# Layer 0's sample values: four of eight samples moved from TensorE to VectorE

## The chip, the core and the metric

The kernel runs on one core of one Trainium2 chip. The time is device microseconds of that core, and the median of three runs is compared. A profile is one execution, taken by the hardware profiler, with every instruction's start and duration. Engines are named as in the profile: PE is TensorE (PEld its weight loads), DVE is VectorE, ACT is ScalarE, POOL is GpSimd, SP is SyncE, whose queue issues nearly all DMAs.

## The reference: what is computed

One inference step of a two-layer decoder. It runs on one prompt of 256 positions and on eight samples, each of one new position with 256 cached ones. Model width is 1024, feed-forward width 2816, and all is float32. Layer 0 mixes block-sparse attention (8 heads of 64) with a gated MLP over 128-position chunks. Layer 1 mixes stick-breaking attention with a causal pooling mixer. Each layer has an input projection, an output projection and a convolutional feed-forward, and every one of these runs for prompt and samples together.

The change touches the attention of the samples. With 256 cached positions, one past block of 256 is always kept, so layer 0's attention of a sample is a softmax over its 256 cached keys and its own key:

```python
past0 = gather_pages(cache_l0_kv, page_table)      # (8, 256, 2, 8, 64)
...
s = jnp.einsum('hqd,hqjsd->hqjs', qh, ks).astype(jnp.float32) * scale
s = jnp.where(mask, s, -jnp.inf)
p = jax.nn.softmax(s.reshape(H, qb, -1), axis=-1).reshape(s.shape)
return jnp.einsum('hqjs,hqjsd->qhd', p.astype(vs.dtype), vs)
```

The last line is the value product: for each sample and head, 256 weights times 256 cached rows of 64 values, plus the sample's own row.

## The kernel before

Tokens lie in columns and features on partitions: 264 columns, 256 of the prompt and 8 of the samples. Every float32 matrix is cut into a high part in TensorE's fast float32 format and the low rest. A product is three matmuls (high by high, high by low, low by high), and the three of one 128x128 weight block are a *block* below. Eight blocks are a *weight tile*. ScalarE makes its high half (`wh`, a copy) and VectorE its low half (`wl`, a subtraction), both in `split`, line 323. At a new tile, `split` traces tiles up to three ahead (`LOOK`), and each half has four buffers, so tile 24 needs the buffer of tile 20. Raw weights come by DMA in chunks of two tiles (`raw`), three chunks deep.

The phases follow each other on TensorE: `in0` (160 blocks, tiles 0 to 19), `out0` (64 blocks, tiles 20 to 27), `ff0`, `dn0`, then `in1`, `out1` (tiles 110 to 117), `ff1`, `dn1`. In an output projection, the first 16 blocks read catB (gated MLP or pooling) for four output tiles. From block 16 on catA (attention) is read, the sample columns included. The attention runs between the blocks: `blk(b, f)` calls `f` after block `b` of the phase. In `in0`, `out0`, `in1` and `out1` TensorE's instructions keep that order (`fixed`). On the other engines a planner orders the instructions before the run. Each engine takes the first in program order of those that the planner's own clock has ready, unless a dependency holds it: `keep_in_program_order` puts an instruction behind the one traced just before it on its engine, and `behind(i, j)` puts `i` behind `j`. `ahead[tt] = (a, b)` makes `split` put tile `tt`'s high half behind `a` and its low half behind `b`. SP's `late` DMAs keep program order.

For the samples, layer 0 does this. `sm_score` makes the scores of all eight, `sm_soft` the softmax (tile `psamp`, rows of heads and samples), `sm_tr` turns the weights and writes them into `PZ`. `sample_av` does the value product on TensorE with 32-column matmuls over two groups of four samples, and ScalarE copies the result into `msk`. In `out0`, `sm_out` turns that back (`po`), adds the own-key part `ob`, and cuts it into catA's sample columns. `v_turn` turns the prompt's values (`vtp`, copied to `vt` by ScalarE and VectorE, half each), `s_av` makes the prompt's attention (`pav`), and `halves` cuts it into catA.

Layer 1 already splits its samples. TensorE does 0 to 3 (`SPE` = 4). For samples 4 to 7, `zs_store` puts the weights into DRAM, `zs_spread` loads them back so that each of the 64 partitions of a head holds that head's 256 weights, and `zs_value` multiplies them with the cached values (laid out with positions along the row) and sums, 16 instructions on VectorE. Large tiles of all kinds share one pool of 24 slots (`up`).

Of the kernel before, what the change touches and what calls it, by code (L numbers as in the profile page):

```python
# [9 lines left out]
F32 = mybir.dt.float32  # L10
# [8 lines left out]
P = 128  # L19
# [144 lines left out]
def _consts():  # L164
# [38 lines left out]
    ("w", ((_NB - 16) * P * P,)), ("xw", (P * (KD + 16 * P + KD * T),)), ("x", (P, KD * T)), ("vec", (P, _NVEC)), ("cst", _CST_ARR.shape), ("rope", (P, 2 * T)), ("edge", (P, 384)),  # L203
    ("kt0", (NPHYS, P, 512)), ("vp0", (NPHYS, P, 512)), ("kt1", (NPHYS, P, 512)), ("vp1", (NPHYS, P, 512)), ("vt1", (NPHYS, P, 512)),
    ("cstate", (P, 2 * NF * 2 * NS)), ("pstate", (P, 4 * NS * 16)),
# [10 lines left out]
def tile_decoder_step(ctx: ExitStack, tc: tile.TileContext, a):  # L216
# [98 lines left out]
    def split(t):  # L315
        for tt in range(len(splits), min(t + (2 if t == 3 else LOOK), NT - 1) + 1):
            ci = chunk_of[tt]
            for c in range(ci, min(ci + 3, len(_CHUNKS))):
                raw(c)
            o = (tt * 8 - coff[ci]) * P  # L320
            src = raws[ci][:, o:o + 8 * P]
            h, l = splits[tt] = wtiles(tt)
            for i, j in zip((s.activation(h, src, AF.Copy), v.tensor_tensor(l, src, h.bitcast(F32), ALU.subtract)), ahead.pop(tt, ())):  # L323
                behind(i, j)
        return splits[t]
# [184 lines left out]

    last = [None]

    def halves(h, l, src, pin=False):
        i = s.activation(h, src, AF.Copy)
        if pin:
            tc.keep_in_program_order(i)
        v.tensor_tensor(l, src, h.bitcast(F32), ALU.subtract)

# [37 lines left out]

    def to_pz(src, fn, groups=2):

        for pg in range(NPG):
            x = src[:, pg * P:(pg + 1) * P].rearrange("p (t x) -> p t x", x=32)[:, :, :2 * NS].rearrange("p t (s c) -> p t s c", c=2)  # L560
            for gr in range(groups):
                s.activation(PZ[:, pg, 4 * gr:4 * gr + 4, NH * gr:NH * gr + NH].rearrange("p s (t c) -> p t s c", c=2), x[:, :, 4 * gr:4 * gr + 4], fn)

    def sample_av(st, pz, vtiles, name, groups=2):
        pv = at(f"pv_{name}")
        for gr in range(groups):
            for pg in range(NPG):
                for j in range(4):
                    sq = 4 * gr + j
                    pe.matmul(pv[32 * j:32 * j + 32, :], pz[:, pg, sq, :], vtiles[sq][:, pg, :],  # L570
                              start=gr + pg == 0, stop=gr + pg == groups + NPG - 2, skip_group_check=True)
        s.activation(st["msk"], pv, AF.Copy)
# [14 lines left out]
    def of_half(x, r):  # L587
        return x.rearrange("p t (g r s) -> p t r s g", g=2, r=2)[:, :, r]

    PZ = con.tile([P, NPG, NS, 32], F32, name="PZ")  # L590
    g.memset(PZ, 0.0)
# [13 lines left out]
    def v_turn(vt, src, ts, name, bank=None, e=None):  # L605
        n = len(ts)
        ps = turn([src[:, t, kb * P:(kb + 1) * P] for kb in range(2) for t in ts], f"vtp_{name}{ts[0]}", bank)
        for r, p in enumerate(ps):
            d, x = vt.rearrange("p b (t r d) -> p b t r d", r=2, d=HF)[:, :, ts[0]:ts[0] + n, r, :], p[:, :2 * n * HF].rearrange("p (b t d) -> p b t d", b=2, t=n)
            v.tensor_copy(d, x) if (e[r] if isinstance(e, tuple) else e) is v else s.activation(d, x, AF.Copy)  # L610

    def p_turn(dst, ws, name, pin=False, e=None, after=None, bank=None):
        ps = turn([w[:, i * P:(i + 1) * P] for w in ws for i in range(3)], name, bank)
        for r, p in enumerate(ps):
            d, x = dst.rearrange("p h (i r d) -> p (h i) r d", r=2, d=HF)[:, :, r, :], p[:, :6 * HF].rearrange("p (x d) -> p x d", d=HF)
            i = v.tensor_copy(d, x) if e is v else s.activation(d, x, AF.Copy)
            if pin:
                tc.keep_in_program_order(i)
            if after is not None:
                behind(i, after)  # L620
# [86 lines left out]
    def pick(xg):  # L707
        return lambda m, k: hl(xg, k)
# [120 lines left out]
    ktiles, kload = page_list(a["kt0"], "K0")  # L829
    vtiles, vload = page_list(a["vp0"], "V0")  # L830
    st0 = {}
# [80 lines left out]
    def sm_out():  # L912
        osam = sm.tile([P, 4, NS], F32, tag="osam", name="osam", bufs=1)
        v.tensor_tensor(osam, st0["ob"], v4[:, :, SEQ:T], ALU.mult)
        for b, r, po in sample_out(st0["msk"], "l0"):
            o = of_half(osam[b:b + 64], r)
            v.tensor_tensor(o, o, po, ALU.add)
        halves(catA[0][:, :, SEQ:T], catA[1][:, :, SEQ:T], osam)
# [45 lines left out]
    def gm_norm():  # L964
        Rb = rstd_of(st0["acc"], 1.0 / 512, "sgu", bank=mmb, w=onesr)
        for t in range(4):
            v.scalar_tensor_tensor(bv4[:, t, :], bv4[:, t, :], vec("sg")[:, t:t + 1], Rb, ALU.mult, ALU.mult)
        bvn = sm.tile([P, 4, NS], F32, tag="bvn", name="bvn", bufs=1)
        g.tensor_copy(bvn, bv4[:, :, SEQ:T])
        nc.sync.dma_start(a["bvn"], bvn)  # L970
        st0["vgt"] = f4("vgt", (P, 2, 512))
# [61 lines left out]
    blk(144, s_tr, 2)  # L1033
    blk(144, s_tr, 3)
    blk(152, gm_own)
    for t in range(4):
        blk(152, gm_gate, t)
    blk(159, lambda: sample_av(st0, PZ, vtiles, "l0"))
    run(orders["in0"], pick(xg), in0_evac, hk)
    nc.sync.dma_start(a["v0"], v4)  # L1040
    hk = Hooks()
    blk(4, sm_out)
    blk(4, lambda: v_turn(vt, v4, range(4), "v0", e=(s, v)))
    for t in range(4):
        blk(9, s_av, t)
# [116 lines left out]
    def zs_tr():  # L1162
        pP = mmb("pP1")
        for pg in range(NPG):
            pe.transpose(pP[:, pg * P:(pg + 1) * P], st1["zs"][:, pg * P:(pg + 1) * P], ident)
        to_pz(pP, AF.Copy, 1)
        st1["msk"] = f4("msk1", (P, 512))
# [6 lines left out]


    zsd = drp.tile([2 * (NS - SPE), 4, PAST], F32, name="zsd")
    spread = {}

    def zs_store():
        for t in range(4):  # L1180
            late(zsd[:, t], st1["zs"][32 * t + 2 * SPE:32 * t + 2 * NS, :])
        st1["osam"] = sm.tile([P, 4, NS], F32, tag="osam", name="osam1", bufs=1)

    def zs_spread(sq):
        pb = spread[sq] = f4(f"pb{sq}", (P, 4, PAST))
        for c in range(2):
            late(pb[64 * c:64 * c + 64], zsd[2 * (sq - SPE) + c].unsqueeze(0).to_broadcast([64, 4, PAST]))

    def zs_value(i):
        sq, t = SPE + i // 4, i % 4  # L1190
        pg = lambda x: x.rearrange("p (g k) -> p g k", g=NPG)
        x = pg(spread[sq][:, t, :])
        j = v.tensor_tensor_reduce(out=x, in0=x, in1=vtiles[sq][:, :, t * P:(t + 1) * P], scale=1.0, scalar=0.0,
                                   op0=ALU.mult, op1=ALU.add, accum_out=st1["osam"][:, t, sq:sq + 1])
        tc.keep_in_program_order(j)
        if i == 15:
            ahead[113] = cast[0], j

# [33 lines left out]
    def pool_mix(t):  # L1232
# [7 lines left out]
        s.activation(hh, pm[:, :T], AF.Copy, scale=gs)  # L1240
        v.scalar_tensor_tensor(ll, pm[:, :T], gs, hh.bitcast(F32), ALU.mult, ALU.subtract)

# [21 lines left out]
    blk(80, zs_score)  # L1264
    blk(93, zs_tr)
    blk(90, zs_store)
    for sq, b in enumerate((98.0, 100.0, 102.0, 106.0)):
        blk(b, zs_spread, SPE + sq)
    values = (107.0, 107.1, 108.0, 109.0, 110.0, 111.0, 112.0, 113.0, 114.0, 120.0, 120.0, 127.9, 127.9, 127.9, 127.9, 127.9)
    for i, b in enumerate(values):  # L1270
        if b < 128:
            blk(b, zs_value, i)
    blk(93, z_qk, 1)
    blk(93, z_tr, 0)
    blk(105, z_tr, 1, True)
    blk(105, z_qk, 2)
    blk(105, lambda: sample_av(st1, PZ, vtiles, "l1", 1))
    blk(117, z_qk, 3)
# [11 lines left out]
    blk(6, lambda: v_turn(vt, v4, range(2, 4), "v1", mmb))  # L1290
    for i, b in enumerate(values):
        if b >= 128:
            blk(b - 128, zs_value, i)
    blk(6, zs_out)
# [62 lines left out]
def _lay(inp):  # L1357
# [17 lines left out]
        "edge": _EDGE,  # L1375
        "kt0": kt(f["cache_l0_kv"]), "vp0": f["cache_l0_kv"][:, :, 1].reshape(NPHYS, P, 512),
        "kt1": kt(f["cache_l1_kv"]), "vp1": f["cache_l1_kv"][:, :, 1].reshape(NPHYS, P, 512), "vt1": kt(f["cache_l1_kv"], 1),
# [47 lines left out]
```

## Time and profile before

| | |
|---|---|
| median of 3 runs | 586.49 us (586.23 to 586.67) |
| the profiled execution | 586.43 us, span 584.7 us |
| TensorE | 577.4 us busy, 99%, mean granted clock 0.997 |
| VectorE | 438.8 us busy, 75% |
| ScalarE | 340.1 us busy, 58% |
| DMA | 124.55 MB, mean 213 GB/s |
| layer 0's `pv` matmuls (start 75.88) | 3.57 us |
| layer 1's `pv` matmuls (start 344.43) | 1.85 us |

In a timeline a row is: start in us, length in us, engine, line, operation, output and inputs with shapes, count; in brackets the engine's idle time before it and what released it. Consecutive instructions overlap at their ends, so the pace of a series is read from start to start. In the chain of waits a row is a stretch of the chain that ended last: start, length, engine and what ran. `CUSTOM_DVE_ANT_1` is VectorE's multiply with a sum (`tensor_tensor_reduce`), and the `READ_ACCUMULATOR` behind it fetches the sum.

### The profile page before, as it was taken

How to read it: one execution, taken by the hardware profiler on the slowest of the kernel's cores; microseconds unless marked ns; L12 is line 12 of the kernel's file. 1: busy time of each engine (PE TensorE's matmuls, PEld its weight loads, DVE VectorE, ACT ScalarE, POOL GpSimd, SP SyncE). 2: the span in 40 equal slices, each digit the busy share in tenths (PEclk: the TensorE clock that was granted, in tenths of full speed). 3: DMA queues.
4: the chain of work that ended last, by engine and by line, in shares of the span. 5: the costliest groups of instructions: out<-in, count | busy, mean ns of one | idle time of the engine just before them, and what ended most of it. 6: DMA issues, size and time to landing. Idle time of an engine off the chain costs nothing.

```text
span 584.7 us, 12461 instructions
## 1 busy us (share of the span) xinstructions
PE 577.4 (99%) x4960; PEld 563.7 (96%) x4960; DVE 438.8 (75%) x812; ACT 340.1 (58%) x602; POOL 45.6 (8%) x62
## 2 busy tenths in 40 slices
PE   9999999999999999999999999999999999999995
PEld 8998979999999999999999889999999999999995
DVE  6999977787877878656669889778787787865561
ACT  7848746665655656544445567667565565664431
POOL 1000123200000000001130000120000000011011
PEclk9999999999999999999999999999999999999998
DMA  8999664454545455995567885645454545454501
GB/s 332 411 355 410 212 222 180 170 213 153 209 156 205 163 200 165 346 319 188 184 226 262 314 262 173 219 168 195 166 206 155 212 154 212 159 209 155 207 1 74
DMA packets 29420, 124.55 MB, mean 213 GB/s; under 512 B 3602, under 2 KB 6578, under 8 KB 17970
## 3 DMA queue, kind: packets, MB, share of 16 engines
q1 hardware_dynamic: 28928, 123.24, 59.0%
q8 instruction: 39, 0.64, 0.4%
q10 hardware_dynamic: 434, 0.51, 0.3%
q14 instruction: 19, 0.16, 0.1%
HBM read 119.75 MB, written 3.99 MB: 212 GB/s over the span
## 4 chain that ended last, share of the span: by engine, by line
PE 97%; issue 1%; DMA 1%; POOLq 0%; ACT 0%; DVE 0%; POOL 0%; ACTq 0%
PE mm L228 90%; PE sc L228 1%; PE pav L228 1%; PE pv_l L228 1%; DMA xw<-in_xw 1%; PE pt L231 1%; PE Z L228 1%; PE S L228 1%; PE pf L228 0%; PE pm L228 0%; POOLq L1400 0%; PE vtp_v L231 0%; PE po_l L231 0%; PE vtp_sgu L231 0%; ACT xg_h L439 0%
## 5 line engine op out<-in xcount | busy, mean ns | idle before, releaser
L323 ACT ACTIVATE wh<-raw 128x1024 fp32r<-128x1024 f32 x177 | 187.5, 1060 | 196.9 <-PE mm L228 191.3
L323 DVE TENSOR_TENSOR wl<-raw,wh 128x1024 fp32r<-128x1024 f32 x177 | 216.9, 1226 | 105.7 <-ACT wh L323 104.7
L228 PE MATMUL mm<-xg_f_h,wh 128*128 128x264 f32 x704 | 199.9, 284 | 0.0
L228 PE MATMUL mm<-xg_f_h,wl 128*128 128x264 f32 x704 | 199.8, 284 | 0.0
L228 PE MATMUL mm<-xg_f_l,wh 128*128 128x264 f32 x704 | 198.6, 282 | 0.0
L228 PEld LDWEIGHTS mm<-xg_f_l,wh 128*128 128x128 f32 x704 | 132.8, 189 | 0.0
L228 PEld LDWEIGHTS mm<-xg_f_h,wh 128*128 128x128 f32 x704 | 132.5, 188 | 0.0
L228 PEld LDWEIGHTS mm<-xg_f_h,wl 128*128 128x128 f32 x704 | 132.4, 188 | 0.0
L228 PE MATMUL mm<-a_h,wh 128*128 128x264 f32 x352 | 100.0, 284 | 0.0
L228 PE MATMUL mm<-a_h,wl 128*128 128x264 f32 x352 | 99.9, 284 | 0.0
L228 PE MATMUL mm<-a_l,wh 128*128 128x264 f32 x352 | 99.3, 282 | 0.0
L228 PEld LDWEIGHTS mm<-a_l,wh 128*128 128x128 f32 x352 | 66.4, 189 | 0.0
L228 PEld LDWEIGHTS mm<-a_h,wh 128*128 128x128 f32 x352 | 66.2, 188 | 0.0
L228 PEld LDWEIGHTS mm<-a_h,wl 128*128 128x128 f32 x352 | 66.2, 188 | 0.0
L228 PE MATMUL mm<-xg_h,wh 128*128 128x264 f32 x160 | 42.5, 290 | 0.3 <-ACT xg_h L439 0.3
L228 PE MATMUL mm<-xg_h,wl 128*128 128x264 f32 x160 | 41.7, 284 | 0.0
L228 PE MATMUL mm<-xg_l,wh 128*128 128x264 f32 x160 | 41.5, 284 | 0.0
L228 PE MATMUL mm<-xg_n_h,wh 128*128 128x264 f32 x128 | 36.8, 288 | 0.0
L228 PE MATMUL mm<-xg_n_h,wl 128*128 128x264 f32 x128 | 36.4, 284 | 0.0
L228 PE MATMUL mm<-xg_n_l,wh 128*128 128x264 f32 x128 | 36.2, 283 | 0.0
L228 PEld LDWEIGHTS mm<-xg_h,wh 128*128 128x128 f32 x160 | 28.6, 188 | 2.0 <-issue 1.2
L228 PEld LDWEIGHTS mm<-xg_l,wh 128*128 128x128 f32 x160 | 28.6, 189 | 0.0
(266 smaller groups left out, 855.7 us busy)
## 6 DMA issues: line engine op xcount, KB each, us to landing
raw<-in_w SPq DMA_DIRECT2D x89, 1024.0 KB, 4.8
K<-in_kt SPq DMA_DIRECT2D x32, 256.0 KB, 5.4
V<-in_vp SPq DMA_DIRECT2D x24, 256.0 KB, 6.0
V<-in_vt SPq DMA_DIRECT2D x8, 256.0 KB, 4.3
pb<-zsd SPq DMA_DIRECT2D x8, 256.0 KB, 6.9
raw<-in_w SPq DMA_DIRECT2D x3, 512.0 KB
xw<-in_xw SPq DMA_DIRECT2D x3, 388.0 KB
X<-in_x SPq DMA_DIRECT2D x8, 132.0 KB, 6.2
```

The costliest lines, as they stand in the source:

```text
L228: return self.keep(nc.tensor.matmul(*x, **k))
L231: return self.keep(nc.tensor.transpose(*x, **k))
L323: for i, j in zip((s.activation(h, src, AF.Copy), v.tensor_tensor(l, src, h.bitcast(F32), ALU.subtract)), ahead.pop(tt, ())):
```

## The change

1. Layer 0's samples 4 to 7 go layer 1's way. The three functions become `spread_of`, used by both layers. `sample_av` and `to_pz` lose their second group, and PZ its second half. The cached values of samples 4 to 7 are loaded from a second layout, `vt0`. The stores stand at block 139 of `in0`, the four loads at 142 to 148. Value 0 stands at block 158, 1 to 6 at 160, 7 to 15 at block 6 of `out0`. The final add and cut of the samples (`sm_cut`) stands at block 12 of `out0`.
2. Three weight tiles are held: tile 21 behind the last `pT` copy, 22 behind the gate's last catB subtraction, 23 behind `vt`'s copy. At tile 20 `LOOK` is 2, so that tile 23 is traced after its hold.
3. The store of `bvn` becomes a `late` DMA at block 156.
4. In layer 1, values 4 to 8 move a little (107, 107.1, 108 to 114 become 107 four times, 112 four times, 116). Tile 111 is held behind the last eviction of the pooling mixer, and `LOOK` is 2 at tile 108.

```diff
-        for tt in range(len(splits), min(t + (2 if t == 3 else LOOK), NT - 1) + 1):
+        for tt in range(len(splits), min(t + (2 if t in (3, 20, 108) else LOOK), NT - 1) + 1):
...
-    def sample_av(st, pz, vtiles, name, groups=2):
+    def sample_av(st, pz, vtiles, name):
         pv = at(f"pv_{name}")
-        for gr in range(groups):
-            for pg in range(NPG):
-                for j in range(4):
-                    sq = 4 * gr + j
-                    pe.matmul(pv[32 * j:32 * j + 32, :], pz[:, pg, sq, :], vtiles[sq][:, pg, :],
-                              start=gr + pg == 0, stop=gr + pg == groups + NPG - 2, skip_group_check=True)
+        for pg in range(NPG):
+            for sq in range(SPE):
+                pe.matmul(pv[32 * sq:32 * sq + 32, :], pz[:, pg, sq, :], vtiles[sq][:, pg, :],
+                          start=pg == 0, stop=pg == NPG - 1, skip_group_check=True)
...
+    def spread_of(name, st, pr, vtiles):
+        zd = drp.tile([2 * (NS - SPE), 4, PAST], F32, name=f"zd_{name}")
+        spread = {}
+
+        def store():
+            for t in range(4):
+                late(zd[:, t], st[pr][32 * t + 2 * SPE:32 * t + 2 * NS, :PAST])
+            st["osam"] = sm.tile([P, 4, NS], F32, tag="osam", name=f"osam_{name}", bufs=1)
+
+        def load(i):
+            pb = spread[i] = f4(f"pb{i}_{name}", (P, 4, PAST))
+            for c in range(2):
+                late(pb[64 * c:64 * c + 64], zd[2 * i + c].unsqueeze(0).to_broadcast([64, 4, PAST]))
+
+        def value(n, then=None):
+            i, t = n // 4, n % 4
+            x = spread[i][:, t, :].rearrange("p (g k) -> p g k", g=NPG)
+            j = v.tensor_tensor_reduce(out=x, in0=x, in1=vtiles[SPE + i][:, :, t * P:(t + 1) * P], scale=1.0, scalar=0.0,
+                                       op0=ALU.mult, op1=ALU.add, accum_out=st["osam"][:, t, SPE + i:SPE + i + 1])
+            tc.keep_in_program_order(j)
+            if n == 15 and then is not None:
+                ahead[then] = cast[0], j
...
     def sm_out():
-        osam = sm.tile([P, 4, NS], F32, tag="osam", name="osam", bufs=1)
-        v.tensor_tensor(osam, st0["ob"], v4[:, :, SEQ:T], ALU.mult)
+        ob = st0["ob"]
+        v.tensor_tensor(ob, ob, v4[:, :, SEQ:T], ALU.mult)
         for b, r, po in sample_out(st0["msk"], "l0"):
-            o = of_half(osam[b:b + 64], r)
-            v.tensor_tensor(o, o, po, ALU.add)
+            v.tensor_copy(of_half(st0["osam"][b:b + 64], r)[..., 0:1], po[..., 0:1])
+
+    def sm_cut():
+        osam = st0["osam"]
+        v.tensor_tensor(osam, osam, st0["ob"], ALU.add)
         halves(catA[0][:, :, SEQ:T], catA[1][:, :, SEQ:T], osam)
...
+    def hold(tt):
+        ahead[tt] = cast[0], held_by[0]
...
+    blk(144, hold, 21)
     blk(152, gm_own)
     for t in range(4):
         blk(152, gm_gate, t)
+    blk(152, hold, 22)
     blk(159, lambda: sample_av(st0, PZ, vtiles, "l0"))
+    blk(156, lambda: late(a["bvn"], st0["bvn"]))
+    sm_store, sm_load, sm_value = spread_of("l0", st0, "ps", vtiles)
+    blk(139, sm_store)
+    for i, b in enumerate((142.0, 144.0, 146.0, 148.0)):
+        blk(b, sm_load, i)
+    late_values = (158.0, 160.0, 160.0, 160.0, 160.0, 160.0, 160.0, 166.0, 166.0, 166.0, 166.0, 166.0, 166.0, 166.0, 166.0, 166.0)
...
     blk(4, sm_out)
+    for i, b in enumerate(late_values):
+        if b > 160:
+            blk(b - 160, sm_value, i)
+    blk(12, sm_cut)
     blk(4, lambda: v_turn(vt, v4, range(4), "v0", e=(s, v)))
+    blk(4, hold, 23)
...
+        i = v.scalar_tensor_tensor(ll, pm[:, :T], gs, hh.bitcast(F32), ALU.mult, ALU.subtract)
+        if t == 3:
+            ahead[111] = cast[0], i
...
-    values = (107.0, 107.1, 108.0, 109.0, 110.0, 111.0, 112.0, 113.0, 114.0, 120.0, 120.0, 127.9, 127.9, 127.9, 127.9, 127.9)
+    for i, b in enumerate((107.0, 107.0, 107.0, 107.0, 112.0, 112.0, 112.0, 112.0, 116.0, 120.0, 120.0, 127.9, 127.9, 127.9, 127.9, 127.9)):
+        blk(b, zs_value, i, 113)
```

More of the change, by code (lines that the diff above doesn't have):

```diff
@@ L203 @@
     ("w", ((_NB - 16) * P * P,)), ("xw", (P * (KD + 16 * P + KD * T),)), ("x", (P, KD * T)), ("vec", (P, _NVEC)), ("cst", _CST_ARR.shape), ("rope", (P, 2 * T)), ("edge", (P, 384)),
-    ("kt0", (NPHYS, P, 512)), ("vp0", (NPHYS, P, 512)), ("kt1", (NPHYS, P, 512)), ("vp1", (NPHYS, P, 512)), ("vt1", (NPHYS, P, 512)),
+    ("kt0", (NPHYS, P, 512)), ("vp0", (NPHYS, P, 512)), ("vt0", (NPHYS, P, 512)), ("kt1", (NPHYS, P, 512)), ("vp1", (NPHYS, P, 512)), ("vt1", (NPHYS, P, 512)),
     ("cstate", (P, 2 * NF * 2 * NS)), ("pstate", (P, 4 * NS * 16)),
@@ L509, in rstd_from @@
         return R
-    last = [None]
+    last, held_by = [None], [None]
     def halves(h, l, src, pin=False):
@@ L516, in halves @@
             tc.keep_in_program_order(i)
-        v.tensor_tensor(l, src, h.bitcast(F32), ALU.subtract)
+        held_by[0] = v.tensor_tensor(l, src, h.bitcast(F32), ALU.subtract)
     def page_list(cache, name, turned=None):
@@ L555, in sample_score, with to_pz @@
                           kt[sq][:, :, t * P:(t + 1) * P], start=sq == 0, stop=sq == NS - 1, skip_group_check=True)
-    def to_pz(src, fn, groups=2):
+    def to_pz(src, fn):
         for pg in range(NPG):
             x = src[:, pg * P:(pg + 1) * P].rearrange("p (t x) -> p t x", x=32)[:, :, :2 * NS].rearrange("p t (s c) -> p t s c", c=2)
-            for gr in range(groups):
-                s.activation(PZ[:, pg, 4 * gr:4 * gr + 4, NH * gr:NH * gr + NH].rearrange("p s (t c) -> p t s c", c=2), x[:, :, 4 * gr:4 * gr + 4], fn)
-    def sample_av(st, pz, vtiles, name, groups=2):
+            s.activation(PZ[:, pg, :, 0:NH].rearrange("p s (t c) -> p t s c", c=2), x[:, :, :SPE], fn)
+    def sample_av(st, pz, vtiles, name):
         pv = at(f"pv_{name}")
-        for gr in range(groups):
-            for pg in range(NPG):
-                for j in range(4):
-                    sq = 4 * gr + j
-                    pe.matmul(pv[32 * j:32 * j + 32, :], pz[:, pg, sq, :], vtiles[sq][:, pg, :],
-                              start=gr + pg == 0, stop=gr + pg == groups + NPG - 2, skip_group_check=True)
+        for pg in range(NPG):
+            for sq in range(SPE):
+                pe.matmul(pv[32 * sq:32 * sq + 32, :], pz[:, pg, sq, :], vtiles[sq][:, pg, :],
+                          start=pg == 0, stop=pg == NPG - 1, skip_group_check=True)
         s.activation(st["msk"], pv, AF.Copy)
@@ L588, in of_half @@
         return x.rearrange("p t (g r s) -> p t r s g", g=2, r=2)[:, :, r]
-    PZ = con.tile([P, NPG, NS, 32], F32, name="PZ")
+    def spread_of(name, st, pr, vtiles):
[17 more added lines that the diff above has]
+                ahead[then] = cast[0], j
+        return store, load, value
+    PZ = con.tile([P, NPG, SPE, 32], F32, name="PZ")
     g.memset(PZ, 0.0)
@@ L609, in v_turn @@
             d, x = vt.rearrange("p b (t r d) -> p b t r d", r=2, d=HF)[:, :, ts[0]:ts[0] + n, r, :], p[:, :2 * n * HF].rearrange("p (b t d) -> p b t d", b=2, t=n)
-            v.tensor_copy(d, x) if (e[r] if isinstance(e, tuple) else e) is v else s.activation(d, x, AF.Copy)
+            if (e[r] if isinstance(e, tuple) else e) is v:
+                held_by[0] = v.tensor_copy(d, x)
+            else:
+                s.activation(d, x, AF.Copy)
     def p_turn(dst, ws, name, pin=False, e=None, after=None, bank=None):
@@ L616, in p_turn @@
             i = v.tensor_copy(d, x) if e is v else s.activation(d, x, AF.Copy)
+            held_by[0] = i
             if pin:
@@ L829, in tile_decoder_step @@
     ktiles, kload = page_list(a["kt0"], "K0")
-    vtiles, vload = page_list(a["vp0"], "V0")
+    vtiles, vload = page_list(a["vp0"], "V0", a["vt0"])
     st0 = {}
@@ L969, in gm_norm @@
         g.tensor_copy(bvn, bv4[:, :, SEQ:T])
-        nc.sync.dma_start(a["bvn"], bvn)
+        st0["bvn"] = bvn
         st0["vgt"] = f4("vgt", (P, 2, 512))
@@ L1037, in tile_decoder_step @@
         blk(152, gm_gate, t)
+    blk(152, hold, 22)
     blk(159, lambda: sample_av(st0, PZ, vtiles, "l0"))
+    blk(156, lambda: late(a["bvn"], st0["bvn"]))
[5 more added lines that the diff above has]
+    for i, b in enumerate(late_values):
+        if b <= 160:
+            blk(b, sm_value, i)
     run(orders["in0"], pick(xg), in0_evac, hk)
@@ L1042, in tile_decoder_step @@
     blk(4, sm_out)
+    for i, b in enumerate(late_values):
+        if b > 160:
+            blk(b - 160, sm_value, i)
+    blk(12, sm_cut)
     blk(4, lambda: v_turn(vt, v4, range(4), "v0", e=(s, v)))
+    blk(4, hold, 23)
     for t in range(4):
@@ L1165, in zs_tr @@
             pe.transpose(pP[:, pg * P:(pg + 1) * P], st1["zs"][:, pg * P:(pg + 1) * P], ident)
-        to_pz(pP, AF.Copy, 1)
+        to_pz(pP, AF.Copy)
         st1["msk"] = f4("msk1", (P, 512))
@@ L1173, in zs_out @@
         halves(catA[0][:, :, SEQ:T], catA[1][:, :, SEQ:T], osam, True)
[L1176 to L1197, printed above, removed]
     PW = 16
@@ L1240, in pool_mix @@
         s.activation(hh, pm[:, :T], AF.Copy, scale=gs)
-        v.scalar_tensor_tensor(ll, pm[:, :T], gs, hh.bitcast(F32), ALU.mult, ALU.subtract)
+        i = v.scalar_tensor_tensor(ll, pm[:, :T], gs, hh.bitcast(F32), ALU.mult, ALU.subtract)
+        if t == 3:
+            ahead[111] = cast[0], i
     def in1_evac(m, o):
@@ L1265, in tile_decoder_step @@
     blk(93, zs_tr)
+    zs_store, zs_load, zs_value = spread_of("l1", st1, "zs", vtiles)
     blk(90, zs_store)
-    for sq, b in enumerate((98.0, 100.0, 102.0, 106.0)):
-        blk(b, zs_spread, SPE + sq)
-    values = (107.0, 107.1, 108.0, 109.0, 110.0, 111.0, 112.0, 113.0, 114.0, 120.0, 120.0, 127.9, 127.9, 127.9, 127.9, 127.9)
-    for i, b in enumerate(values):
-        if b < 128:
-            blk(b, zs_value, i)
+    for i, b in enumerate((98.0, 100.0, 102.0, 106.0)):
+        blk(b, zs_load, i)
+    for i, b in enumerate((107.0, 107.0, 107.0, 107.0, 112.0, 112.0, 112.0, 112.0, 116.0, 120.0, 120.0, 127.9, 127.9, 127.9, 127.9, 127.9)):
+        blk(b, zs_value, i, 113)
     blk(93, z_qk, 1)
@@ L1276, in tile_decoder_step @@
     blk(105, z_qk, 2)
-    blk(105, lambda: sample_av(st1, PZ, vtiles, "l1", 1))
+    blk(105, lambda: sample_av(st1, PZ, vtiles, "l1"))
     blk(117, z_qk, 3)
@@ L1290, in tile_decoder_step @@
     blk(6, lambda: v_turn(vt, v4, range(2, 4), "v1", mmb))
-    for i, b in enumerate(values):
-        if b >= 128:
-            blk(b - 128, zs_value, i)
     blk(6, zs_out)
@@ L1375, in _lay @@
         "edge": _EDGE,
-        "kt0": kt(f["cache_l0_kv"]), "vp0": f["cache_l0_kv"][:, :, 1].reshape(NPHYS, P, 512),
+        "kt0": kt(f["cache_l0_kv"]), "vp0": f["cache_l0_kv"][:, :, 1].reshape(NPHYS, P, 512), "vt0": kt(f["cache_l0_kv"], 1),
         "kt1": kt(f["cache_l1_kv"]), "vp1": f["cache_l1_kv"][:, :, 1].reshape(NPHYS, P, 512), "vt1": kt(f["cache_l1_kv"], 1),
```

## The prediction, made before the result was known

> **What bounds the kernel now.** I read the page first, then the chain of waits, then the timelines of single engines around the edit.
>
> ```profile
> PE 97%; issue 1%; DMA 1%; POOLq 0%; ACT 0%; DVE 0%; POOL 0%; ACTq 0%
> ```
>
> TensorE is 97% of the chain that ended last. So only two things move the end: TensorE work that goes away, and stalls that TensorE gets or loses. The profiled execution took 586.43 us, its span and what lies around it; the median of the runs is 586.49, so a sum made against the former needs no correction.
>
> The chain of waits in order of time (start, length, what), around the edit:
>
> ```profile
> 75.88 3.57 PE pv_l L228 x32
> ...
> 81.87 0.50 PE vtp_v L231 x16
> 82.38 2.02 PE mm L228 x15
> 84.40 2.80 PE pav L228 x32
> 87.20 25.76 PE mm L228 x211
> ...
> 344.43 1.85 PE pv_l L228 x16
> ...
> 350.13 0.61 PE pm L228 x3
> ...
> 351.47 0.37 PE pm L228 x3
> ```
>
> Every step here is TensorE's own: in this stretch it waits for nobody. A block of three matmuls takes 25.76/211*3 = 0.366 us, which converts block numbers of the program into time.
>
> VectorE is what the edit loads. Two windows (second number on is PE, PEld, DVE, ACT, POOL busy; then clock, DMA share, GB/s):
>
> ```profile
> 61.31:77.90 16.59, 16.59 (x167) 14.63 (x169) 15.72 (x35) 10.25 (x22) 2.92 (x4) 1.00 0.65 230
> 77.90:89.78 11.88, 11.88 (x123) 9.91 (x116) 6.27 (x14) 4.86 (x9) 3.95 (x6) 1.00 0.54 188
> ```
>
> VectorE is full until 77.90 and has 5.6 us free in the 11.88 us after it. 89.78 is where TensorE first reads catA, the attention half of layer 0's output projection:
>
> ```profile
> 89.78 0.28 PE L228 MATMUL mm<-catA_h,wh 128*128 128x264 f32 x1
> ```
>
> VectorE's own order in that stretch:
>
> ```profile
> 73.61 1.22 DVE L323 TENSOR_TENSOR wl<-raw,wh 128x1024 fp32r<-128x1024 f32 x1
> ...
> 76.78 1.12 DVE L517 TENSOR_TENSOR catB_l<-bu,catB_h 128x264 fp32r<-128x264 f32 x3
> 80.05 0.43 DVE L827 TENSOR_TENSOR v<-mm,R_n 128x264 f32<-128x264 f32 x1 [2.15 <-PE mm L228]
> 80.52 0.19 DVE L914 TENSOR_TENSOR osam<-ob,v 128x32 f32<-128x32 f32 x1
> 81.17 1.23 DVE L323 TENSOR_TENSOR wl<-raw,wh 128x1024 fp32r<-128x1024 f32 x1 [0.46 <-ACT wh L323]
> 82.31 0.78 DVE L917 TENSOR_TENSOR osam<-osam,po_l 64x16 f32<-64x16 f32 x4
> 83.39 0.19 DVE L517 TENSOR_TENSOR catA_l<-osam,catA_h 128x32 fp32r<-128x32 f32 x1 [0.29 <-ACT catA_h L514]
> 83.61 0.69 DVE L610 COPY vt<-vtp_v 128x512 f32<-128x512 f32 x1
> 85.05 1.47 DVE L323 TENSOR_TENSOR wl<-raw,wh 128x1024 fp32r<-128x1024 f32 x1 [0.74 <-ACT wh L323]
> 86.44 1.64 DVE L517 TENSOR_TENSOR catA_l<-pav,catA_h 128x256 fp32r<-128x256 f32 x4
> ```
>
> The weight-tile subtractions at 73.61, 81.17 and 85.05 are tiles 22, 23 and 24. catA is complete at 88.08, 1.70 us before its reader.
>
> **What goes away.** Layer 0's value product loses 8 of 16 matmuls, two of its four rounds of four. Layer 1 already runs the halved form: 1.85 us against 3.57. TensorE saves 1.72 us, all on the chain. The four PZ copies on ScalarE become two, off the path.
>
> **What is added.** Sixteen multiply-and-sum instructions on VectorE, whose pace layer 1 shows (VectorE's timeline there):
>
> ```profile
> 348.17 0.42 DVE L1193 CUSTOM_DVE_ANT_1 pb<-pb,V 128x256 f32<-128x256 f32 x1
> 348.51 0.08 DVE L1193 DVE_READ_ACCUMULATOR2_ANT osam<- 128x1 f32 x1
> 348.51 0.42 DVE L1193 CUSTOM_DVE_ANT_1 pb<-pb,V 128x256 f32<-128x256 f32 x1
> ...
> 362.13 1.22 DVE L323 TENSOR_TENSOR wl<-raw,wh 128x1024 fp32r<-128x1024 f32 x1
> 363.26 0.71 DVE L1172 COPY osam<-po_l 64x8 f32<-64x8 f32 x4
> 364.00 1.23 DVE L323 TENSOR_TENSOR wl<-raw,wh 128x1024 fp32r<-128x1024 f32 x1
> 365.15 0.19 DVE L517 TENSOR_TENSOR catA_l<-osam,catA_h 128x32 fp32r<-128x32 f32 x1
> ```
>
> Start to start is 0.345 us (the accumulator read hides under the next), so 16 cost 5.5 us; a tile subtraction is 1.14 to the next start, four sample copies 0.71. One 0.2 us add is new (sm_cut). Nothing of this lies under a wait of VectorE before 77.9, since the first value is pinned behind tile 22's subtraction and values 1 to 6 behind the last v eviction.
>
> **Where it lands.** I lay VectorE out by these starts, in the program's order, which is also how both layers run now (in layer 1 above: tile, copies, tile, then catA). Tile 22 is held behind the gate's evictions: they end 1.14 earlier, at 76.8, tile 22 at 77.9. It is first used by block 16 of the output projection (87.2 + 7 blocks in the old time), so holding it costs nothing. Value 0 to 78.2. TensorE's last v block ends 1.72 earlier, v evicted 78.33 to 78.7. Values 1 to 6 to 80.75, the own-key product to 80.95, the four copies to 81.65, vt's half to 82.3. vtp ends at 81.87 + 0.50 - 1.72 = 80.65, in time. pav, due at 84.40 - 1.72 = 82.7, just doesn't wait (holding tile 23 behind vt keeps it so). Values 7 to 15, pinned behind vt, run 9*0.345 = 3.1, to 85.4. Then tile 23 to 86.5 and tile 24 to 87.65: both are traced at block 8 of the projection, ahead of pav's evictions at block 9, and neither is held behind the values. Then four catA_l subtractions at 0.345 to 89.0, the add, ScalarE's sample cut (0.3 with its handoff) and VectorE's: 89.6. TensorE now wants catA at 89.78 - 1.72 = 88.06. So the stall that I expect is 1.55 us, at block 16 of layer 0's output projection.
>
> **GpSimd beside it.** In the same stretch GpSimd prepares the convolution (its timeline):
>
> ```profile
> 85.39 1.47 POOL L645 TENSOR_TENSOR C<-CSTATE,VEC 128x176 f32<-128x176 f32 x1
> ```
>
> Tile 24's subtraction, which runs beside the 1.47, took 1.47 instead of 1.23; I add 0.24 once, for whichever two-input instruction meets it. The state load is issued after v's store, 1.72 earlier, so the spell falls on values 8 to 15. The Trainium skill, GPSIMD Engine Reference, section Specifications, has GpSimd's SBUF interfaces shared with VectorE and names contention for instructions with two SBUF inputs. By that rule each value, with two such inputs, would be slowed; at the 20% of the row above nine values cost 0.6 instead of 0.24, and the sum would be 0.4 more. Only one overlapping pair shows it here.
>
> **The DMAs.** The spread goes through DRAM: psamp, 63.9, then four stores, then eight loads on SP's queue. Rows of VectorE's timeline, of SP's in layer 1, of the times to landing there and of SP's waits:
>
> ```profile
> 63.49 0.36 DVE L894 TENSOR_SCALAR psamp<-psamp,sts 128x257 f32<-128x257 f32 x1
> 346.34 1.08 SPq L291 DMA_DIRECT2D pb<-zsd  x2
> DMA to landing us min/median/max: 3.7/6.9/10.1
> SPq L291 <- DMA zsd<-zs: 2.7, 2, 2.6
> ```
>
> Stores 63.9 to 65.4, a wait of 2.6, loads from 68 at 0.54 each (1.08 for two): the first pair lands at about 76, the fourth at about 79 to 83. Value 0 is due at 77.9 and value 12 at 84.0, so they fit with little over. SP waits at the store and at the loads, with residual inputs and one weight chunk queued behind; chunks are three ahead, so TensorE doesn't see it. bvn's store, which stood in front of the last value pages, now stands behind the loads. Price: nothing, if the fourth pair gets its buffer; otherwise the third rival.
>
> **Layer 1.** The pm at 350.13 lasts 0.61 where its neighbours last 0.37: a wait of 0.24, of which the matmul after it starts 0.13 late beyond the usual step. Evicting pm ahead of the values and tile 111 should remove 0.13; bounds 0 to 0.24. Tile 111's first use is 7 us later. The value that holds tile 113 stays last. I count -0.13.
>
> **Sum.** 586.43 - 1.72 - 0.13 + 1.55 + 0.24 = 586.4: the saved matmuls are given back as a wait for VectorE. Bounds of this case: contention 0 to 0.6 and the last handoff, 0.3 either way, so 585.9 to 587.0.
>
> **Rivals.**
>
> 1. *No stall.* If the planner sets pav's evictions ahead of tiles 23 and 24, catA is ready at 85.4 + 1.4 + 0.6 = 87.4, before 88.06. For it: tile 23's first use, block 24 at 91, leaves room. Against: in both layers the tile traced earlier went first (85.05 before 86.44; 364.00 before 365.15). Time 586.43 - 1.85 = 584.6.
> 2. *One tile ahead.* If only tile 24 slips behind catA, the stall is 1.79 - 1.14 = 0.65: 585.2. For it: tile 24 waits for tile 20's buffer, and so starts latest.
> 3. *The fourth spread pair is late: slower.* Large tiles share 24 slots; in layer 1 the last pair was issued only at 346.34, when the value product had ended (344.43 + 1.85) and freed pages. If layer 0 does the same, the pair goes at 75.88 + 1.85 = 77.7, is issued by 78.9 and lands after 6.9 at 85.8, at worst at 89. Values 12 to 15 are pinned, and vt's tile, catA and two weight tiles stand behind them on VectorE. From 84.0 on each microsecond counts fully: 1.8 late makes 588.2. Against: layer 0's eight key pages are free from 60 on.
> 4. *Holding a tile starves TensorE*: tile 23, done at 86.5 and due at 91, has 4 us; no time.
>
> **How the numbers follow.** About 0.2%, 1.2 us, is what a measurement of this kernel can tell from no change. Forecast 0.53, first rival 0.19, second 0.13, third 0.13, the rest unnamed. The first rival and about half of the second lie below 585.3: with a little from the forecast's lower tail, faster 0.31. Slower is the third rival and a little of the forecast's upper tail: 0.15. Same 0.54. The range takes in the first rival below and ends at 587.7 above, inside the third.
>
> **What would show it.** Right: pv_l at 16 records and about 1.85 us; TensorE's chain with a VectorE piece of 1 to 2 us ahead of the first catA matmul, and two weight-tile subtractions between the last value and the pav evictions. Wrong: catA_l complete before TensorE's block 16 (rivals 1, 2); an idle VectorE between values 11 and 12 put down to a DMA (rival 3); any stall at vtp or pav, which would mean that the values went ahead of vt.

## The result: slower, and outside the forecast's range

The changed kernel took 593.25 us (median of 6 runs, 589.08 to 597.01) where the kernel before took 586.54 in the same comparison: a ratio of 1.0105, 95% interval [1.0076, 1.0134]. The runs of the kernel before lie within 0.5 us of each other; those of the changed kernel spread over 8 us. So there are two questions: where the fastest of them, the profiled one (589.08 us, span 587.3), lost 2.6 us, and what makes four of the other five 4 to 8 us longer still.

The chain of waits of the changed kernel, profiled after the change (start, length, what):

```profile
76.33 1.85 PE pv_l L228 x16
...
81.10 2.02 PE mm L228 x15
83.12 2.80 PE pav L228 x32
85.92 2.63 PE mm L228 x20
...
88.58 1.07 ACT wh L323
...
89.67 1.38 DVE wl L323
91.06 0.41 DVE catA_l L517
...
91.51 24.60 PE mm L228 x189
...
117.20 191.57 PE mm L228 x1589
...
356.93 0.25 PE vtp_v L231 x8
...
369.46 25.03 PE mm L228 x205
```

The value product is halved to the 1.85 us that was forecast, vtp and pav wait for nothing, and then TensorE, in its 20 records from 85.92 on, runs out of work at 88.5. Behind it stand a cast of ScalarE, a tile subtraction and a piece of catA_l. The two engines' own order there, first VectorE's timeline, then ScalarE's:

```profile
85.42 0.42 DVE L604 CUSTOM_DVE_ANT_1 pb_l<-pb_l,V 128x256 f32<-128x256 f32 x1
...
85.77 2.35 DVE L323 TENSOR_TENSOR wl<-raw,wh 128x1024 fp32r<-128x1024 f32 x2
88.04 0.75 DVE L517 TENSOR_TENSOR catA_l<-pav,catA_h 128x256 fp32r<-128x256 f32 x2
88.71 0.18 DVE L946 TENSOR_TENSOR osam_l<-osam_l,ob 128x32 f32<-128x32 f32 x1
88.81 0.75 DVE L517 TENSOR_TENSOR catA_l<-pav,catA_h 128x256 fp32r<-128x256 f32 x2
89.67 1.38 DVE L323 TENSOR_TENSOR wl<-raw,wh 128x1024 fp32r<-128x1024 f32 x1
90.98 0.47 DVE L517 TENSOR_TENSOR catA_l<-osam_l,catA_h 128x32 fp32r<-128x32 f32 x1
```

```profile
88.58 1.06 ACT L323 ACTIVATE wh<-raw 128x1024 fp32r<-128x1024 f32 x1 [2.24 <-PE mm L228]
89.55 0.21 ACT L514 ACTIVATE catA_h<-osam_l 128x32 fp32r<-128x32 f32 x1
```

Up to 88.81 this is the forecast's layout, 0.4 us late with the whole program: tiles 23 and 24 ahead of pav's evictions. What it had not foreseen is tile 25. Its cast stands on ScalarE ahead of the last cast of catA_h and waits 2.24 us for a matmul to free its buffer; that matmul is among the last ones ahead of catA. So TensorE stops, tile 25 is cast and subtracted (1.06 and 1.38 us), and only then come the sample columns of catA, which TensorE needs to go on. In the program's order tile 25, traced at block 16, stands behind the samples' cut at block 12; the planner put it first all the same. In the kernel before, the cast of tile 25 waited for TensorE just as long, but the samples' cut had long been done, at 83.39 (ScalarE's timeline before):

```profile
89.92 1.06 ACT L323 ACTIVATE wh<-raw 128x1024 fp32r<-128x1024 f32 x1 [2.30 <-PE mm L228]
```

After the change, TensorE's timeline gives the two gaps, and the windows what lies around them (columns: length, PE, PEld, DVE, ACT and POOL busy, granted clock, DMA share, GB/s):

```profile
88.38 0.28 PE L228 MATMUL mm<-catB_h,wl 128*128 128x264 f32 x1
89.81 0.39 PE L228 MATMUL mm<-catA_h,wh 128*128 128x264 f32 x1 [1.15 <-ACT catA_h L514]
91.51 0.39 PE L228 MATMUL mm<-catA_l,wh 128*128 128x264 f32 x1 [1.31 <-DVE catA_l L517]
...
92.49 0.42 PE L228 MATMUL mm<-catA_l,wh 128*128 128x264 f32 x1
92.71 0.42 PE L228 MATMUL mm<-catA_h,wl 128*128 128x264 f32 x1
```

```profile
76.00:84.00 8.00, 8.00 (x84) 5.92 (x84) 7.65 (x33) 3.42 (x6) 0.00 (x0) 1.00 1.06 265
84.00:88.00 4.00, 4.00 (x41) 3.72 (x38) 4.00 (x14) 1.52 (x4) 0.00 (x0) 1.00 0.83 329
...
92.00:96.00 4.00, 4.00 (x23) 4.00 (x22) 0.92 (x2) 0.83 (x2) 1.05 (x2) 0.57 0.94 365
```

Start to start, 88.38 to 89.81 and 89.81 to 91.51, less a matmul's 0.12 each: a stall of 1.31 + 1.58 = 2.89 us. Behind it the matmuls start 0.22 us apart (92.49, 92.71) instead of 0.12, and the granted clock of that window is 0.57. Before the change no window there was below 1.00.

The profiled execution adds up. At pav's end it is 85.92 - 87.20 = -1.28 against the kernel before: 1.72 won, 0.44 lost ahead of it, 0.27 of that in the first 20 us. At the first feed-forward it is 117.20 - 114.05 = +3.15, so 4.43 were lost between: 2.89 of stall, 1.43 of low clock (24.60 us for the 189 matmuls where a run of them with the full clock takes 23.17, below), 0.1 of start-up. At layer 1's output projection it is 369.46 - 366.55 = +2.91, so layer 1 won 0.24; 0.3 more came back at the end.

### The profile page after: what moved, and what is told of

Its sections match the earlier page's. It is cut to its first block, busy times and chain, and to the rows that moved or that the text cites. A ratio compares the mean times of both kernels' runs of the same rounds, so it can differ in the third digit from the quotient of the medians.

```text
span 587.3 us, 12481 instructions
## 1 busy us (share of the span) xinstructions
PE 577.3 (98%) x4944; PEld 564.5 (96%) x4944; DVE 444.0 (76%) x845; ACT 340.3 (58%) x600; POOL 45.9 (8%) x62
## 4 chain that ended last, share of the span: by engine, by line
PE 86%; DVE 5%; ACT 3%; issue 2%; DMA 2%; POOLq 0%; SPq 0%; POOL 0%; ACTq 0%
PE mm L228 82%; DVE wl L323 2%; DMA xw<-in_xw 2%; ACT p L883 1%; PE pav L228 1%; ACT wh L323 1%; PE pv_l L228 1%; PE sc L228 1%; PE Z L228 1%; ACT wh L766 0%; PE pt L231 0%; DVE sqw L791 0%; ACT p L889 0%; DVE rz_q L842 0%; DVE rz_k L842 0%
## 5 line engine op out<-in xcount | busy, mean ns | idle before, releaser
L323 ACT ACTIVATE wh<-raw 128x1024 fp32r<-128x1024 f32 x177 | 187.7, 1062 | 196.9 <-PE mm L228 189.5
```

## Which tile makes the stall

My first theory was that weight tiles ahead of catA make the stall; its rivals were layer 1's edits and the spread through DRAM. First the changed kernel again, unchanged:

> The changed kernel unaltered, for another of its executions, since its times lie between 589.1 and 597.0 us. Theory A (the two weight tiles 23 and 24, and tile 25 after them, stand ahead of catA's last piece on VectorE and ScalarE; TensorE idles 3 us and then runs at a lower granted clock): the same wait of 2.5 to 4 us at catA is seen, and whatever else this execution loses lies behind it in stretches of lower clock. Rival B (DMAs of the spread make weights or values late by a varying amount): the extra time lies in waits of VectorE, ScalarE or TensorE put down to a DMA, ahead of or behind catA.

It took 594.3 us. Its stall was longer, 3.95 us, since the fourth pair of spread transfers landed late (VectorE's timeline):

```profile
85.59 0.42 DVE L604 CUSTOM_DVE_ANT_1 pb_l<-pb_l,V 128x256 f32<-128x256 f32 x1 [1.27 <-DMA pb_l<-zd_l]
```

That is the forecast's third rival, in part of the executions and at 1.3 us. Its chain holds more, to which I come back:

```profile
92.44 24.86 PE mm L228 x189
...
118.41 195.09 PE mm L228 x1589
```

Then all three tiles held:

```diff
-min(t + (2 if t in (3, 20, 108) else LOOK), NT - 1)
+min(t + (1 if t == 21 else 2 if t in (3, 20, 108) else LOOK), NT - 1)
...
-        halves(catA[0][:, :, SEQ:T], catA[1][:, :, SEQ:T], osam)
+        i = s.activation(catA[0][:, :, SEQ:T], osam, AF.Copy)
+        j = v.tensor_tensor(catA[1][:, :, SEQ:T], osam, catA[0][:, :, SEQ:T].bitcast(F32), ALU.subtract)
+        ahead[23], ahead[24], ahead[25] = (cast[0], j), (cast[0], j), (i, j)
...
-    blk(4, hold, 23)
```

> The changed kernel with tiles 23, 24 and 25 held behind catA's sample cut (tile 23 no longer behind vt). Theory A: the wait at catA falls from 3.1 us to under 0.7, no stretch of lower clock follows, and the time is 584.6 to 585.6 us, steady within 1 us. Rival B: the time stays between 588 and 597 and keeps its spread of several us.

584.65 us (584.28 to 585.07, 5 runs), ratio to the kernel before 0.9966 [0.9952, 0.998]. It beats both kernels: the 1.72 us are kept. Its chain has no wait between pav and the feed-forward:

```profile
82.86 2.80 PE pav L228 x32
85.66 25.76 PE mm L228 x211
```

The other two do one part each on the kernel before: layer 1's edits (tile 111 behind the evictions, the values' due times) and layer 0's spread (its stores and loads and the moved store of bvn, the landed values unread).

> The kernel before with the layer 1 part alone (value places, tile 111 held, the shorter look-ahead at tile 108). Both theories: 586.0 to 586.6 us; the pm matmul's wait of 0.13 to 0.24 goes or moves, nothing else.

> The kernel before with only the DMAs of layer 0's spread added (four stores, eight loads that nothing reads) and bvn's store moved; the values of all eight samples stay on TensorE. Theory A: 586.3 to 587.0 us, no spread of times. Rival B: 588 us or more, with a spread of several us as in the changed kernel.

Layer 1's part: 586.65 us, ratio 0.9992 [0.9976, 1.0009], no difference that the times can show. The spread alone: 587.18 us, ratio 1.0033 [1.0002, 1.0064], 0.6 us; two of its ten runs were at 591.4 and 595.2. Its trace puts the loss ahead of the value product: from the samples' transposes (pP) to pv_l it is 11.68 us (65.03 to 76.71) where it is 10.75 in the kernel before (65.13 to 75.88) and in the changed one (65.58 to 76.33). The planner had set tile 21's subtraction, which waits for its cast, ahead of vgt, which TensorE needs next (VectorE's timeline, before and then with the spread alone):

```profile
68.08 1.27 DVE L610 COPY vgt<-vtp_sgu 128x512 f32<-128x512 f32 x2
...
69.22 1.23 DVE L323 TENSOR_TENSOR wl<-raw,wh 128x1024 fp32r<-128x1024 f32 x1 [1.34 <-ACT wh L323]
70.36 1.28 DVE L610 COPY vgt<-vtp_sgu 128x512 f32<-128x512 f32 x2
```

The changed kernel holds tile 21, and its trace does not show this loss.

To part the tiles, the changed kernel with tile 25 alone held (as above, but only `ahead[25] = i, j`, tile 23's own hold left in), and a kernel that was meant to hold tiles 23 and 24 alone:

> The changed kernel with tile 25 alone held: its cast on ScalarE and its subtraction on VectorE go behind the last pieces of catA; tiles 23 and 24 stay ahead of catA as the change left them. Theory A (tile 25 made the part of the stall that was not foreseen, since its cast waits for TensorE's last matmul ahead of catA and catA's last cast is queued behind it): TensorE's idle time at catA falls from about 2.9 us to 1.3 to 1.8 us, the forecast's own; the granted clock stays at 1.00 in the stretch after it; 585.8 to 587.0 us, and all executions within 1 us of each other. Rival S (the long executions come with the spread transfers, not with the stall): the same middle, but executions from 590 to 597 us among them. Rival T (tiles 23 and 24 make the stall, tile 25 adds nothing): stall and clock drop stay, 589 us and above.

> The changed kernel with tiles 23 and 24 held behind the last pieces of catA, tile 25 left ahead of them as the change left it. Theory A: tile 25's cast can't start before TensorE's last matmul ahead of catA (about 88.5 us), takes 1.06 us, its subtraction 1.2 to 1.4 us, and catA's last pieces stand behind both, so the stall stays at 2.6 to 3.1 us although VectorE has nothing else to do: 589 us where the matmul step returns to 0.1205 us, 592 to 595 us where it stays at 0.123 us up to layer 1. Rival T (tiles 23 and 24 make the stall): no stall, 584.7 us.

With tile 25 held the profiled execution took 586.19 us, and its stall was 1.38 + 0.59 - 2*0.12 = 1.73 us; no low clock. VectorE's timeline there shows tiles 23 and 24 ahead of catA, as forecast, but also a wait of 0.47 us for the fourth spread pair, on which everything behind it hangs:

```profile
84.65 0.42 DVE L604 CUSTOM_DVE_ANT_1 pb_l<-pb_l,V 128x256 f32<-128x256 f32 x1 [0.47 <-DMA pb_l<-zd_l]
...
86.03 2.35 DVE L323 TENSOR_TENSOR wl<-raw,wh 128x1024 fp32r<-128x1024 f32 x2
88.31 0.75 DVE L517 TENSOR_TENSOR catA_l<-pav,catA_h 128x256 fp32r<-128x256 f32 x2
```

The edit of the second kernel does not do what was meant. It sets the holds at block 12, but without the shorter look-ahead at tile 21 tiles 23 and 24 are traced at block 8, ahead of that, so the holds never apply. With its old hold gone, tile 23 runs ahead of the sample copies, and tile 24 still runs ahead of catA (VectorE's timeline):

```profile
81.10 1.22 DVE L323 TENSOR_TENSOR wl<-raw,wh 128x1024 fp32r<-128x1024 f32 x1
...
86.68 1.22 DVE L323 TENSOR_TENSOR wl<-raw,wh 128x1024 fp32r<-128x1024 f32 x1
...
89.14 0.57 DVE L946 TENSOR_TENSOR osam_l<-osam_l,ob 128x32 f32<-128x32 f32 x1
90.27 1.23 DVE L323 TENSOR_TENSOR wl<-raw,wh 128x1024 fp32r<-128x1024 f32 x1 [0.55 <-ACT wh L323]
```

The stall was (1.43 + 1.60 - 0.24) 2.79 us, nearly the 2.89 of the changed kernel, although one tile less stood ahead of catA and VectorE stood idle for 0.55 us ahead of tile 25. So tile 25 sets the stall, and without it tiles 23 and 24, with the late pair, make 1.73: the two don't add, they overlap. No run has tile 25 ahead of catA with both other tiles held. (This kernel also lost 0.8 us at pav, since tile 23 delayed vt.) The clock stayed at 1.00 behind this stall, which gives the full-clock time of the 189 matmuls (its chain):

```profile
92.01 23.17 PE mm L228 x189
```

The times, though, fit neither theory: medians 587.45 (585.59 to 593.43, 10 runs) and 590.65 (587.44 to 594.32, 6 runs). The first was to lie within 1 us; 4 of its 10 runs are above 590.

## What the stall costs beyond its length

The rivals now: the clock and the matmul step react to the stall (theory C), or the long executions come from the spread transfers (rival S). The kernel before, with nothing of the change, gets a stall made by useless VectorE instructions, 8 or 12:

```diff
         halves(catA[0][:, t, :SEQ], catA[1][:, t, :SEQ], pav[:, :SEQ])
+        c = catA[1][:, t, :SEQ]
+        for _ in range(12 if t == 0 else 0):
+            ahead[25] = cast[0], v.tensor_tensor(c, c.bitcast(F32), c.bitcast(F32), ALU.max)
```

> The kernel before with 8 more VectorE instructions (each replaces a part of catA_l by the greater of itself and itself, so nothing changes in value) ahead of TensorE's first matmul with catA_l, tile 25's subtraction behind them; nothing of the change in it. By 0.35 to 0.43 us each, TensorE idles 0.9 to 1.6 us. Theory C (the granted clock falls and the matmul step lengthens only after an idle stretch of about 3 us): 587.4 to 588.2 us, all executions within 0.7 us, clock 1.00 after the stall. Rival S (the spread transfers make the long executions): the same.

> The same with 12 such instructions: TensorE idles 2.3 to 3.3 us in the kernel before, without any of the change. Theory C: the granted clock falls to about 0.57 for 3 to 4 us behind the stall, which costs 1.4 us beside the 2.3 to 3.3 us, 590 to 591.5 us, and in some executions the matmul step stays at 0.123 us for some 250 us, another 4 to 5 us. Rival S (the spread transfers make the long executions, and the low clock too): only the idle time is added, 588.8 to 589.8 us, all executions within 0.7 us.

With 8: a stall of 1.43 us, clock 1.00 behind it, 588.61 us (587.5 to 592.68, 10 runs), more than the 588.2 that both theories allowed. With 12: a stall of 3.27 us, 592.91 us (591.34 to 595.7, 4 runs), ratio 1.0098 [1.0081, 1.0115]. The low clock is there without a single part of the change (windows of the kernel before with 12):

```profile
92.00:96.00 4.00, 2.71 (x15) 2.71 (x16) 2.73 (x5) 0.00 (x0) 0.00 (x0) 0.75 0.19 31
```

From 0.7 us behind the gap the matmuls started 0.22 us apart, for 3.4 us. The Trainium skill, TensorE: Matmul & The Clock Gate, section What's actually happening, says that the clock of the array is halved after about one idle window of 3.4 us, on a window that runs freely, and is whole again after one busy window. The traces agree on about the half (0.22 against 0.12 us) and on the length of the penalty. On the idle time they differ from the Trainium skill: stalls of 2.85 and 2.89 us, shorter than that window and with one matmul in the middle, brought it, as did 3.27, 3.35 and 3.95 us; stalls of 2.79 and 3.1 did not, nor did 1.4 to 1.9 (five traces). So near 3 us the length alone does not decide; what does is not shown.

The profiled execution of the kernel with 12 took 595.7 us. Its chain:

```profile
93.29 24.96 PE mm L228 x189
...
119.36 195.09 PE mm L228 x1589
...
375.82 25.03 PE mm L228 x205
```

195.09 us for the 1589 matmuls of the first feed-forward, the same as in the 594.3 us execution above, against 191.57: 0.1228 us each instead of 0.1206, with a granted clock of 1.00 throughout. This is the second part of the loss: 3.5 us there and some 0.8 us around it. The step keeps one value from a restart of TensorE to the attention of layer 1. VectorE and ScalarE keep their pace (over a whole run a tile's subtraction takes 1224 to 1228 ns and its cast 1060 to 1062 ns, in both kinds of execution).

More traces were needed to see what a long execution holds: of the kernel with tile 25 held, of the kernel with 8, and of the best kernel (tiles 23, 24 and 25 held), which was also timed again.

> The kernel with tile 25 alone held, once more, for the trace of another execution: 4 of its 10 lay at 590 us and above. Theory C (a granted clock that falls, or a longer matmul step, behind the stall): a long execution shows the stall of 1.3 to 2 us and behind it steps of 0.22 us or of 0.123 us; values 12 to 15 do not wait. Rival S (the fourth pair of spread transfers lands late): values 12 to 15 wait on VectorE by 1 us or more, the stall is longer by as much, and the step is 0.1205 us behind it. A short execution, 585.5 to 587 us, shows neither.

> As the run before it, a third execution of the same kernel; the theories expect the same of it.

> The kernel before with 8 more VectorE instructions, once more: its profiled execution had a stall of 1.45 us and took 587.8 us, most others 588.5 to 589.4. Theory C: the stall is the same 1.45 us, and what is longer lies behind it, as matmul steps of 0.22 us for up to 3.4 us or of 0.123 us. Rival (the stall itself varies): the gap ahead of the first matmul with catA_l is 2 us or more, and the step is 0.1205 us behind it.

> The changed kernel with tiles 23, 24 and 25 held behind the last pieces of catA, as in the run of that name, with more rounds: 584.3 to 585.1 us. Theory C: with no stall at catA no execution has a low clock behind it, so nearly all lie within 1 us, as the kernel before's do. Rival S (the spread transfers make the long executions): one in five or more at 589 us and above.

The first execution, 586.98 us, took 192.44 us for the 1589 matmuls, a third value of the step (0.1211 us). The second was long, 590.64 us; its stall was 1.41 + 0.47 = 1.88 us, its fourth spread pair 0.6 us late, its clock 1.00, and its chain:

```profile
90.12 23.46 PE mm L228 x189
...
114.68 195.09 PE mm L228 x1589
```

So the long step needs no low clock. The third, 590.29 us, showed a stall of 1.60 us and the step of 0.1211 us again, in the second feed-forward too (177.80 us for 1468 matmuls against 177.03). In the best kernel (584.81 us, 584.17 to 590.12, 12 runs; ratio 0.9975 [0.9959, 0.9991]) ten runs lie within 1.3 us and two at 588.8 and 590.1. The profiled one is the 588.8, and has the long step with hardly a stall (its chain, then TensorE's and VectorE's timelines):

```profile
85.64 26.17 PE mm L228 x211
...
112.92 195.09 PE mm L228 x1589
```

```profile
88.34 0.39 PE L228 MATMUL mm<-catA_l,wh 128*128 128x264 f32 x1
88.57 0.29 PE L228 MATMUL mm<-catA_h,wl 128*128 128x264 f32 x1
```

```profile
85.28 0.43 DVE L604 CUSTOM_DVE_ANT_1 pb_l<-pb_l,V 128x256 f32<-128x256 f32 x1 [1.10 <-DMA pb_l<-zd_l]
...
88.10 0.19 DVE L948 TENSOR_TENSOR catA_l<-osam_l,catA_h 128x32 fp32r<-128x32 f32 x1
```

The late spread pair is here too, 1.10 us, so catA's last piece ends at 88.29, just as TensorE comes to it. The matmul at 88.34 shows a restart, as those behind the stalls do: it lasts 0.39 us, and the next starts 0.23 later instead of 0.12. That is a wait of 0.11 us, and the long step follows: the 211 matmuls took 0.41 us more than 25.76, this 0.11 and the 0.30 by which the 189 behind catA were longer in the 590.64 us execution (23.46 against 23.16 in the 586.19 one). So theory C falls in the form that it takes a stall of several us, and rival S in the form that a late transfer makes a long execution by its own wait.

What the 17 traces leave is this. All four with the long step have it behind a wait of TensorE at catA, of 0.11 to 3.95 us, and none of the four without such a wait has it. But six with a wait of 1.4 to 3.35 us kept 0.1206. Among the ten traces of kernels that use the spread, the step goes with VectorE's wait for the fourth pair: 0.1206 us in the four without one, 0.1206, 0.1211 and 0.1211 at 0.42 to 0.48 us, and 0.1228 in all three at 0.62 to 1.27. That is a lead and not a cause, since the kernel with 12 has the long step and no spread.

To see what a typical execution of the changed kernel holds, and how often a stall alone brings the long step:

> The changed kernel, unchanged, for the trace of one more execution: its times go from 589 to 597 us, and the two traces so far (589.1 and 594.3) differ in the matmul step behind the stall. Theory C: the stall at catA is 2.7 to 4 us in each; an execution near 593 us has the 1589 matmuls of the first feed-forward in 195.1 us (0.123 us each), one near 589 to 590 us in 191.6 us. Rival S (a long execution is one whose fourth spread pair lands late): values 12 to 15 wait 3 us or more in a long one, and the 1589 matmuls take 191.6 us.

> As the run before it: the same kernel, a further execution, the same expectations.

> The kernel before with 12 more VectorE instructions ahead of catA_l, once more for its spread: four executions so far, 591.3 to 595.7 us. Theory C1 (a stall with the low clock behind it brings the long step by itself): half of the executions or more at 595 us and above. Theory C2 (the stall alone does it seldom; in the changed kernel the spread transfers add to it): a quarter or fewer, the rest at 591 to 593 us.

Both executions of the changed kernel were short ones, 588.84 us (stall 2.85, low clock, step 0.1206) and 588.34 us (stall 3.1, no low clock, step 0.1211). The kernel with 12 took 592.07 us (591.03 to 593.53, 4 runs), none long. Counting as long what lies 3.5 us or more above the fastest execution of the same kernel:

```
                                           long / all executions
stall and spread (changed kernel, tile 25
   held, tile 23 let go)                     5/9 + 5/12 + 3/6 = 13/27
stall, no spread (8 or 12 instructions)      1/11 + 1/8       =  2/19
spread, no long stall (spread alone, best)   2/10 + 2/17      =  4/27
neither (before, layer 1 alone)              1/71 + 0/10      =  1/81
```

With both it is every second execution, which is what lifts the changed kernel's median from 589 to 593. The spread without a long stall stands above the last row; 2 of 19 are too few to say so of the stall alone. The one long execution of the changed kernel that was profiled (594.3) had the long step; for the other four there are only times, three near 593.5 us, which the step's 4.3 us fit, and 597.0, which needs more. What sets the step, and why it comes oftener with spread transfers and a stall, stays open: no run tells.

## Why the prediction was wrong, point by point

- *What goes away*: right. pv_l fell from 3.57 to 1.85 us in 16 records, and nothing waited at vtp or pav.
- *Where it lands*: right in its order as far as it went. The values run at 0.345 us, the nine behind vt end at 85.8, tiles 23 and 24 go next and pav's evictions follow, so rivals 1 and 2 are out. The reason that I gave for it, that the tiles are traced earlier, is not the one: with tile 25 held they are traced at block 16, behind the evictions, and still go first. That kernel's stall of 1.73 us and its 586.19 us come close to the forecast's 1.79 and 586.4, but partly by luck: 0.47 of the 1.73 is the wait for the fourth spread pair, which I had at nothing. Without it I estimate 1.26 us (1.73 - 0.47), and the two tiles took their usual 2.35 us, with no slowing by GpSimd.
- *The step that failed* is the sum's stall term, "So the stall that I expect is 1.55 us". I laid VectorE out up to tile 24, in the program's order, and left ScalarE to a handoff of 0.3. In that order tile 25 comes behind the samples' cut; the planner, which takes what its own clock has ready, had it ahead. Tile 25's cast stood on ScalarE ahead of catA_h's last piece and could not start before TensorE had nearly come to catA; its subtraction did the same on VectorE. The term measured 2.89 us instead of 1.79.
- *The second failure* is that I priced a stall at its length. Behind 2.89 us the granted clock fell to 0.57 and cost 1.43 more, and the step of the next 1950 matmuls can settle at 0.1228 us, 4.3 us more, by the times in about half of the executions. No term of mine stood for either. The longer stall alone would have given 587.5 us (586.4 + 2.89 - 1.79), just inside the range that ended at 587.7; these two took the result out of it.
- *GpSimd*: the row was right, the neighbour wrong. The state load landed late, GpSimd stood idle beside the values (POOL 0.00 from 84 to 88), and its 1.47 us instruction met tile 25: 1.38 instead of 1.23, so 0.15 for my 0.24, inside the stall. Whether the Trainium skill's shared interfaces (GPSIMD Engine Reference, Specifications) would slow the values is not shown by any run.
- *The DMAs, rival 3*: the fourth pair did land late in some executions, 1.27 us in the 594.3 one and 0.4 to 1.1 in others, under a DMA share of 1.06 from 76 to 84 in the changed kernel, where it was 0.56 before. I gave it 0.13 for an outcome that turned out to be an addition to the forecast rather than an alternative. "Nothing" for the spread itself held in the profiled execution of the changed kernel, where no value waited, and failed wherever the pair was late.
- *Layer 1*: the pm wait that I wanted removed is still there: in the changed kernel the pm at 353.27 lasts 0.60 us and its neighbours 0.36. What went is a wait at vtp: 0.25 us now (356.93 above), where the chain of the kernel before has

```profile
353.79 0.43 PE vtp_v L231 x8
```

  With what follows it, 0.24 us in the trace instead of 0.13, too little for the times to show.
- *Rival 4*, a held tile starving TensorE: right that it doesn't. Holding tiles 23, 24 and 25 behind catA is what made the best kernel.

## What to carry over

When work moves to an engine with slack, lay out every in-order engine up to the moment its reader starts, ScalarE as well, by the order that the planner takes and not by the program's, and look for a prefetch whose buffer is freed by the very matmuls that come before the wait: it turns being late into a circle. Hold such prefetches behind what TensorE needs next. And price a TensorE stall near 3 us at more than its length, since the clock behind it may be halved for 3.4 us; then compare several executions, not one.

## What I had not expected of the hardware

- The step of back-to-back matmuls of 128x264 took one of three values, 0.1206, 0.1211 or 0.1228 us, kept over up to 250 us, all at a granted clock of 1.00. All four traced stretches of the longest began behind a wait of TensorE, once of only 0.11 us.
- A stall of about 3 us is enough for the granted clock to halve, with one matmul in the middle of it too, but not each time.
- In the changed kernel GpSimd's state load arrived 4.5 us later than before (its first instruction at 89.04 instead of 84.49), though it was issued earlier (79.75 instead of 80.91). With the spread alone that instruction came at 90.31, so the delay comes with the spread's transfers.
